# Half of the output projection's early products between the last attention steps, and the attention's PSUM pool kept through the projection

## The chip, the cores and the metric

The kernel runs on one core of one Trainium2 chip. The time of a run is the device time of one execution in microseconds (us); lower is better. A core has a matrix engine (TensorE, "PE" in the profile), a vector engine (VectorE, "DVE"), an activation engine (ScalarE, "ACT"), a general engine (GpSimd, "POOL") and a queue engine that mostly starts transfers (SyncE, "SP"). Each takes its own instructions strictly in the order of its queue. Matrix products land in PSUM, which has eight banks; one bank holds 512 float32 values in each of 128 partitions.

## The reference

One decoder block on 1024 tokens of width 1024: eight heads of attention with forgetting beside a gated chunk mixer, an output projection with a residual, and a gated MLP with a causal convolution of width 3.

```python
def block(x):
    xn = rmsnorm(x, norm_mix_g)
    proj = xn @ w_in                      # q, k, v, u, v_gate, forget logits
    att = forgetting_attention(q, k, v, log_sigmoid(f + b_forget))   # 8 heads of 64
    sg = chunked_spatial_gating(gelu(u), gelu(v_gate), ...)
    h = x + concat(att, sg) @ w_out       # the output projection
    h = h + conv_ffn(rmsnorm(h, norm_ffn_g), w_up, conv_w, conv_b, w_down)
    return rmsnorm(h, norm_final_g)
```

The half of `w_out` that belongs to `sg` is multiplied during the attention, and its sum with `x` is kept in the DRAM buffer `hpd`. What follows the attention is the other half, `att @ w_out[:512]`, which is called the projection here.

## The kernel before

**Number format.** Each float32 operand is split into a high and a low part, and each product is three matrix instructions: high by high, high by low, low by high (L1279, L1280, L1281 in `wmm`). A split is a cast (high) and a subtraction (low).

**Stages.** Attention goes head by head, h = 0 to 7, in five steps each (`STEPS`, n = 5h + s, so n = 35 to 39 are the last head's values). In a step PE transposes probabilities (L1026), ACT and DVE split them (L1027, L1028), PE multiplies them with the values (L1042), and ACT and DVE take the values out of PSUM (L1050, L1051). The logits of the next head are made in the same steps (L978, L979) and read by DVE (L991). The order of PE's attention instructions is chained by hand through `seq`; the rest is put in order by a scheduler, engine by engine, by its own estimates.

**The row tail of a head.** The reciprocals of a head's row sums (`rs`) are transposed by PE (L940), copied by ACT (L941), written to the DRAM buffer `rsd` (L942) and loaded again, spread over partitions, by SP (L943). With them `pair_half` normalizes two heads at a time into `attT[k]`, k = 0 to 3: a multiplication (L952 on POOL, L956 on DVE for the last pair), a cast (L953) and a subtraction (L954, L958). The last pair, k = 3, needs the last head.

**The projection.** `wo_load` fetches the four pieces of `w_out` and POOL splits them (L1098, L1099; buffers `whl` for k = 0, 1 and `G` for k = 2, 3). For the token tiles 0, 4, 1 and 5 (`first`) the products over k = 0, 1, 2 are made ahead, 8 tiles of one bank (`banks8`) by 9 instructions, 72 in all: these are the early products. Then, for each token tile in the order 0, 4, 1, 5, 2, 3, 6, 7: `hload` fetches the tile of `hpd` (SP, L1285, into a buffer `pt`), k = 3 follows (or all of k for tiles 2, 3, 6, 7), `hadd` adds bank and tile on DVE (L1289), `norm2` takes the mean square on ACT (L1296, L1297), the reciprocal (L1298) and the scaled tile `xn` on DVE (L1299), and one tile later `flip` transposes `xn` on PE into two banks (L1317). A flip of tiles 0 to 3 is split (ACT L1306, DVE L1303) and copied (ACT L1323); a flip of tiles 4 to 7 is taken out by one copy on ACT (L1328) and two subtractions on DVE (L1329, L1330), and combined further (L1331, L1334).

**The up stage** multiplies sums of quarter blocks (`xB`, `xT`) with the MLP's weights in 12 instructions per bank (L1372). Its first four products, `qa`, stand around `flip(7)`. DVE splits the weights of these first products (L166) right after the last pair's normalization.

**Banks.** A PSUM pool belongs to a stage. `psb`, the attention's, gives two tiles of two banks each for logits (`place()`, tag "L", taken in turn) and four single banks (`bank()`). In the kernel before it is released right after the attention, and the pool of the projection and of the up stage, `psc`, is made of two groups of four single banks (`bank()` and `sbank()`): the early products lie in all eight, flips in `sbank()`, and the up stage's products in both. A tile of a new pool waits for whoever last used the bank.

Of the kernel before, what the change touches and what calls it, by code (L numbers as in the profile page):

```python
# [14 lines left out]
P = 128  # L15
# [54 lines left out]
def block_kernel(ctx: ExitStack, tc: tile.TileContext, xT, xtok, wuv, wv0, wva, wvk, wvl, wqk, cpk, bfv,  # L70
# [1030 lines left out]

    STEPS = [[(h, g) for g in GROUPS[n:n + 2]] for h in range(8) for n in range(0, 9, 2)]
# [35 lines left out]
    for n, step in enumerate(STEPS):  # L1138
# [3 lines left out]
        if h == 7 and s == 0:  # L1142
            for _ in filler:
                pass
            wo_load((0, 1))
            wo_load((2, 3))
        if h in (2, 4, 6) and s == 4:
            for o in (slice(0, 512), slice(512, 1024)):
                pair_half(h // 2 - 1, o)
        now, turned = turned, [turn_p(g) for g in STEPS[n + 1]] if n + 1 < len(STEPS) else []  # L1150
# [25 lines left out]
        fill((h, s))  # L1176
        for _ in range(min(len(SPLIT), 1 if n == 9 else 2)):
            ws_, k, wr = SPLIT.pop(0)
            wt = sb("whl", [P, 2, 512], F32R)
            ws_[k] = wt  # L1180
            after(tc, act.copy(wt[:, 0], wr), out_copy or casts[-1])
            pool.tensor_tensor(out=wt[:, 1], in0=wr, in1=f32(wt[:, 0]), op=ALU.subtract)
# [19 lines left out]
    psa.release()  # L1202
    psa = tc.alloc_tile_pool(name="psc", bufs=4, space=bass.MemoryType.PSUM, reuse_waits="tile")
# [71 lines left out]
    def wmm(tt, hf, ps, ks_):  # L1275
        ts_ = slice(tt * P, (tt + 1) * P)
        for k in ks_:
            w = wo[k][hf]
            pe.matmul(ps, attT[k][:, 0, ts_], w[:, 0, :], start=(k == 0), stop=False)  # L1279
            pe.matmul(ps, attT[k][:, 0, ts_], w[:, 1, :], start=False, stop=False)  # L1280
            pe.matmul(ps, attT[k][:, 1, ts_], w[:, 0, :], start=False, stop=(k == 3))  # L1281

# [26 lines left out]
    def flip(tt):  # L1309
# [3 lines left out]
        for kh in range(2):  # L1313
            ps = sbank()
            for j in range(4):
                k = 4 * kh + j
                pe.transpose(ps[:, j * P:(j + 1) * P], xn[tt][:, k * P:(k + 1) * P], ident)  # L1317
            pp.append(ps.rearrange("p (k t) -> p k t", k=4))
# [44 lines left out]
    for n in ("T1", "T4", "B22"):  # L1363
        xb_tile(upr, n)

# [15 lines left out]
    for i in range(AHEAD):  # L1381
# [4 lines left out]
        if i == 0:  # L1386

            last = flip(7)
# [430 lines left out]
```

## Time and profile before

| | |
|---|---|
| median of 3 runs | 1050.03 us (1049.67 to 1050.81) |
| the profiled execution | 1049.46 us; its span, first to last instruction, 1047.7 us |
| busy over the span | PE 1038.1, DVE 892.0, ACT 562.3, POOL 218.7 us |
| last head's steps end, early products begin (PE) | 360.78 us from the span's start |
| first product of the up stage (PE) | 410.22 us |
| granted TensorE clock, mean | 0.999 |

Rows of the timeline read: start in us from the span's start, duration in us, engine, line, operation, output and inputs by the program's names, partitions x elements, type, count, and in brackets the idle time of the engine just before, with what ended it. Matrix instructions are pipelined, so that the duration of one overlaps the next; the distance between two starts is what one costs. Rows of the windows give, for a stretch of time, the busy time of each engine with the number of instructions in parentheses, then the granted clock of PE, the share of the transfer engines and GB/s.

### The profile page before, as it was taken

The numbers are of one execution on the slowest core, as the hardware profiler recorded it, in microseconds if no ns is written. First come the engines' busy times: TensorE is split into PE (matmuls) and PEld (weight loads), VectorE is DVE, ScalarE is ACT, GpSimd is POOL, SyncE is SP. The second block draws the span as 40 slices with busy tenths as digits, with TensorE's granted clock in tenths as the row PEclk, the third lists the DMA queues.
The fourth block names the chain that finished last, engine by engine and source line by source line (L and its number), as shares of the span: only waits on it lengthen the run. The fifth ranks groups of instructions, "written<-read, shape, count | busy, mean of one in ns | idle before, by whom it ended". The sixth has DMA issues, their size and how long they took to land.

```text
span 1047.7 us, 14269 instructions
## 1 busy us (share of the span) xinstructions
PE 1038.1 (99%) x4998; PEld 869.6 (83%) x4998; DVE 892.0 (85%) x1302; ACT 562.3 (54%) x1003; POOL 218.7 (21%) x165
## 2 busy tenths in 40 slices
PE   9999999999999999999999999999999999999997
PEld 6988888988888888788888888888888888888886
DVE  6899887888888779998999989898997866997774
ACT  6777632457767747744444444444444544454654
POOL 0000241500422540353334323323331000000000
PEclk9999999999999999999999999999999999999999
DMA  9622558785745533232254431432422999333432
GB/s 323 236 91 86 159 154 252 222 256 172 206 137 171 189 134 141 80 105 77 98 173 162 130 124 60 132 120 70 131 81 81 319 331 303 105 99 101 144 118 100
DMA packets 67452, 161.66 MB, mean 154 GB/s; under 512 B 8095, under 2 KB 9239, under 8 KB 67381
## 3 DMA queue, kind: packets, MB, share of 16 engines
q1 hardware_dynamic: 67108, 160.72, 47.8%
q8 instruction: 39, 0.64, 0.3%
q14 instruction: 33, 0.26, 0.1%
q10 hardware_dynamic: 272, 0.04, 0.0%
HBM read 115.68 MB, written 45.05 MB: 153 GB/s over the span
## 4 chain that ended last, share of the span: by engine, by line
PE 87%; DVE 4%; DMA 3%; ACT 3%; issue 1%; POOL 1%; SPq 0%; ACTq 0%; DVEq 0%; POOLq 0%
PE k L1632 20%; PE qc L1372 11%; PE qa L1372 11%; PE qd L1372 11%; PE qb L1372 5%; PE pb L1042 3%; PE ps L270 3%; PE pb L1026 2%; PE qc L510 2%; PE qa L510 2%; PE pb L270 2%; PE qd L510 2%; PE pl L979 2%; PE pl L978 2%; PE pf L1066 1%; PE pf L1067 1%
## 5 line engine op out<-in xcount | busy, mean ns | idle before, releaser
L1632 PE MATMUL k<-whb,wha 128*128 128x512 f32 (+1 forms) x936 | 209.9, 387 | 0.0
L1632 PEld LDWEIGHTS k<-whb,wha 128*128 128x128 f32 x936 | 174.1, 188 | 35.9 <-DVE wha L166 0.2
L1372 PE MATMUL qc<-xT,whb 128*128 128x512 f32 x540 | 129.8, 389 | 0.2 <-ACT whb L160 0.2
L1372 PE MATMUL qa<-xB,wha 128*128 128x512 f32 x528 | 127.4, 390 | 0.0
L1372 PEld LDWEIGHTS qc<-xT,whb 128*128 128x128 f32 x540 | 101.3, 188 | 21.6 <-ACT whb L160 0.6
L1372 PEld LDWEIGHTS qa<-xB,wha 128*128 128x128 f32 x528 | 98.8, 188 | 20.8 <-DVE wha L166 0.4
L160 ACT CAST wha<-sg 128x512 fp32r<-128x512 f32 x77 | 47.7, 621 | 96.8 <-PE k L1632 83.8
L160 ACT CAST whb<-sg 128x512 fp32r<-128x512 f32 x82 | 50.6, 618 | 87.5 <-PE qc L1372 67.3
L166 DVE TENSOR_TENSOR wha<-sg,wha 128x512 fp32r<-128x512 f32 x77 | 52.9, 690 | 38.9 <-ACT wha L160 38.6
L1372 PE MATMUL qd<-xB,whb 128*128 128x512 f32 x264 | 63.7, 389 | 0.0
L1372 PE MATMUL qd<-xT,whb 128*128 128x512 f32 x264 | 63.7, 390 | 0.0
L1372 PE MATMUL qb<-xT,whb 128*128 128x512 f32 x252 | 61.0, 390 | 0.0
L166 DVE TENSOR_TENSOR whb<-sg,whb 128x512 fp32r<-128x512 f32 x82 | 57.1, 698 | 4.4 <-ACT whb L160 4.3
L1027 ACT CAST pt<-pb 128x512 fp32r<-128x512 f32 x72 | 40.4, 584 | 37.5 <-PE pb L1026 32.5
L1256 POOL TENSOR_TENSOR sg<-raw 128x512 f32<-128x512 f32 x20 | 31.2, 1561 | 140.3 <-DVE whb L166 79.9
L1372 PEld LDWEIGHTS qd<-xT,whb 128*128 128x128 f32 x264 | 49.5, 188 | 10.5 <-DVE u L1479 0.3
L1372 PEld LDWEIGHTS qd<-xB,whb 128*128 128x128 f32 x264 | 49.6, 188 | 10.3
L1028 DVE TENSOR_TENSOR pt<-pb,pt 128x512 fp32r<-128x512 f32 x72 | 47.4, 688 | 10.6 <-ACT pt L1027 10.3
L1372 PEld LDWEIGHTS qb<-xT,whb 128*128 128x128 f32 x252 | 47.2, 188 | 10.0 <-DVE whb L166 0.3
L1042 PE MATMUL pb<-pt,V 128*128 128x512 f32 (+3 forms) x192 | 49.6, 362 | 0.4 <-DVE pt L1028 0.3
L1259 POOL TENSOR_TENSOR sg<-sg,raw 128x512 f32<-128x512 f32 x20 | 33.3, 1667 | 63.4 <-DVE whb L166 63.4
L1257 POOL TENSOR_TENSOR sg<-sg,raw 128x512 f32<-128x512 f32 x20 | 34.8, 1742 | 47.5 <-issue 44.9
(424 smaller groups left out, 2242.9 us busy)
## 6 DMA issues: line engine op xcount, KB each, us to landing
raw<-wup SPq DMA_DIRECT2D x44, 512.0 KB
sg<-hx SPq DMA_DIRECT2D x77, 256.0 KB
hx<-hs SPq DMA_DIRECT2D x44, 256.0 KB
hx<-ca SPq DMA_DIRECT2D x35, 256.0 KB
xT<-wdn SPq DMA_DIRECT2D x28, 256.0 KB
x<-kd SPq DMA_DIRECT2D x24, 256.0 KB
A<-xtok SPq DMA_DIRECT2D x8, 512.0 KB
raw<-wqk SPq DMA_DIRECT2D x8, 512.0 KB
```

Source lines behind the costliest of these rows:

```text
L160: act.copy(h, src)
L166: return eng.tensor_tensor(out=l, in0=src, in1=f32(h), op=ALU.subtract)
L270: pe.matmul(banks[m], xs(n, xi, k)[:, ms], w[:, wi, :], start=(first and k == 0 and c == 0 and (own or m % 2 == 0)), stop=(k == 3 and c == ...
L510: pe.matmul(ps, w[:, wi, ks], xs(n, xi, k), start=(first and c == 0), stop=(c == 11), skip_group_check=True)
L1027: casts.append(act.copy(pt[:, 0, :], ptr))
L1028: los.append(dve.tensor_tensor(out=pt[:, 1, :], in0=ptr, in1=f32(pt[:, 0, :]), op=ALU.subtract))
L1042: seq(pe.matmul(po[half][:, o:o + w], lhs, pt[:, s, c:c + w], start=(new and s == 0), stop=(s == 1 and (half, k) in ((1, 6), (0, 3))), ski ...
L1256: pool.tensor_tensor(out=s[0], in0=a21, in1=a22, op=ALU.add)
L1257: pool.tensor_tensor(out=s[1], in0=s[0], in1=a11, op=ALU.add)
L1259: pool.tensor_tensor(out=s[3], in0=s[1], in1=a12, op=ALU.add)
L1372: pe.matmul(ps, w[:, wi, ks], xb[:, xi, k, :], start=(first and n == 0), stop=(n == 11), skip_group_check=True)
L1632: pe.matmul((banks[bk + m] if ps is None else ps)[:, o], xh[:, xi, ms], wh[:, wi, o], start=((first and p_ == 0 or new) and n == 0), stop= ...
```

## The change

Half of the early products, those of token tiles 0 and 4 (36 of 72 instructions), are issued inside the attention's last steps, n = 34 to 38, by a table `EARLY`: each entry is (token tile, half, pieces k). They are chained into PE's order by `seq`. Their banks are the logits' two wide tiles, which the last logits have left by then. The pieces k = 0, 1 of `w_out` are loaded two steps earlier (n = 33 in place of 35), and k = 2, 3 one step earlier (n = 34). The pool `psb` is kept until the projection is over: the early products of tiles 1 and 5 and all later ones use its four single banks, a flip uses a wide tile in place of two single banks, and `psc` is made only before the first up product. `flip(7)` gets two banks of `psc`.

```diff
+    def wmm(tt, hf, ps, ks_, order=lambda m: m):
+        ts_ = slice(tt * P, (tt + 1) * P)
+        for k in ks_:
+            w = wo[k][hf]
+            order(pe.matmul(ps, attT[k][:, 0, ts_], w[:, 0, :], start=(k == 0), stop=False))
+            order(pe.matmul(ps, attT[k][:, 0, ts_], w[:, 1, :], start=False, stop=False))
+            order(pe.matmul(ps, attT[k][:, 1, ts_], w[:, 0, :], start=False, stop=(k == 3)))
+
+    EARLY = {34: ((0, 0, (0, 1)), (0, 1, (0, 1))), 35: ((4, 0, (0, 1)),), 36: ((4, 1, (0, 1)),),
+             37: ((0, 0, (2,)), (0, 1, (2,))), 38: ((4, 0, (2,)), (4, 1, (2,)))}
+    wide, banks8 = {}, {}
...
-        if h == 7 and s == 0:
+        if n == 33:
             for _ in filler:
                 pass
             wo_load((0, 1))
-            wo_load((2, 3))
         if h in (2, 4, 6) and s == 4:
             for o in (slice(0, 512), slice(512, 1024)):
                 pair_half(h // 2 - 1, o)
+        if n == 34:
+            wo_load((2, 3))
...
         fill((h, s))
+        for tt, hf, ks_ in EARLY.get(n, ()):
+            if tt not in wide:
+                wide[tt] = place()
+            banks8[tt, hf] = wide[tt][:, hf * 512:hf * 512 + 512]
+            wmm(tt, hf, banks8[tt, hf], ks_, seq)
...
     early.release()
-    psa.release()
-    psa = tc.alloc_tile_pool(name="psc", bufs=4, space=bass.MemoryType.PSUM, reuse_waits="tile")
...
-    def flip(tt):
+    def flip(tt, two=None):
 
         c = slice((tt % 4) * P, (tt % 4) * P + P)
         pp = []
-        for kh in range(2):
-            ps = sbank()
+        if two is None:
+            t = place()
+            two = [t[:, 0:512], t[:, 512:1024]]
+        for kh, ps in enumerate(two):
...
     first = (0, 4, 1, 5)
-    banks8 = {(tt, hf): (bank() if hf == 0 else sbank()) for tt in first for hf in range(2)}
     for hf in range(2):
-        for tt in first:
+        for tt in first[2:]:
+            banks8[tt, hf] = bank()
             wmm(tt, hf, banks8[tt, hf], (0, 1, 2))
...
     for n in ("T1", "T4", "B22"):
         xb_tile(upr, n)
+    psa.release()
+    psa = tc.alloc_tile_pool(name="psc", bufs=4, space=bass.MemoryType.PSUM, reuse_waits="tile")
...
-            last = flip(7)
+            last = flip(7, [sbank(), sbank()])
```

In the changed kernel the lines lie a little lower: the three products of `wmm` are L1106 to L1108, `hload` L1293, `hadd` L1297, the mean square, root, reciprocal and scaling of `norm2` L1304 to L1307, the subtraction of a split L1311, the transposes of a flip L1327, its copies L1333 and L1338, its subtractions L1339 and L1340, and the up stage's product L1384.

Three places show what moves. First, PE in the last head's steps. The names are `pb`, a single bank, `pl`, a wide tile, `pt`, the split probabilities, `V`, the values, `whl` and `A`, the pieces of `w_out` and of the attention's output. Before, values of one step are followed at once by the transposes of another:

```order
L1042 MATMUL pb_3759<-pt_3692,V_1733 128x512 x2
L1042 MATMUL pb_3759<-pt_3700,V_1733 128x512 x2
L1026 MATMUL pb_3766<-ident,H_3600 128x128 x2
L1026 MATMUL pb_3766<-ident,H_3563 128x128 x2
L1026 MATMUL pb_3774<-ident,H_3600 128x128
L1026 MATMUL pb_3774<-ident,H_3563 128x128 x3
```

In the changed kernel:

```order
L1042 MATMUL pb_3772<-pt_3722,V_1733 128x512 x2
L1042 MATMUL pb_3772<-pt_3730,V_1733 128x512 x2
L1106 MATMUL pl_3779<-whl_3656,A_2849 128x512
L1107 MATMUL pl_3779<-whl_3656,A_2849 128x512
L1108 MATMUL pl_3779<-whl_3656,A_2849 128x512
L1106 MATMUL pl_3779<-whl_3664,A_3281 128x512
L1107 MATMUL pl_3779<-whl_3664,A_3281 128x512
L1108 MATMUL pl_3779<-whl_3664,A_3281 128x512
L1026 MATMUL pb_3786<-ident,H_3600 128x128 x2
L1026 MATMUL pb_3786<-ident,H_3563 128x128 x2
```

Six early products of token tile 4 stand between; five such groups are put in, of 12, 6, 6, 6 and 6 instructions.

Second, PE at the end of the projection, where `flip(6)`, `flip(7)` and the first up products (`qa`) stand. Before:

```order
L1280 MATMUL pb_4270<-G_3738,G_3837 128x512
L1281 MATMUL pb_4270<-G_3738,G_3837 128x512
L1372 MATMUL qa_4318<-xB_3859,wha_3870 128x512 x3
L1317 MATMUL ps_4290<-ident,xn_4232 128x128 x4
L1317 MATMUL ps_4295<-ident,xn_4232 128x128 x4
L1372 MATMUL qa_4318<-xB_3859,wha_3870 128x512 x9
L1372 MATMUL qa_4331<-xB_3860,wha_3873 128x512 x12
L1317 MATMUL ps_4344<-ident,xn_4284 128x128 x4
L1317 MATMUL ps_4349<-ident,xn_4284 128x128 x4
L1372 MATMUL qa_4371<-xB_3859,wha_3956 128x512 x12
```

In the changed kernel:

```order
L1107 MATMUL pb_4258<-G_3716,G_3875 128x512
L1108 MATMUL pb_4258<-G_3716,G_3875 128x512
L1327 MATMUL pl_4278<-ident,xn_4221 128x128 x8
L1384 MATMUL qa_4309<-xB_3893,wha_3904 128x512 x12
L1384 MATMUL qa_4322<-xB_3894,wha_3907 128x512 x12
L1327 MATMUL ps_4335<-ident,xn_4272 128x128 x4
L1327 MATMUL ps_4336<-ident,xn_4272 128x128 x4
L1384 MATMUL qa_4362<-xB_3893,wha_3950 128x512 x12
```

The three products ahead of `flip(6)` now stand behind it, and `flip(6)` lies in the wide tile `pl_4278`. Its two banks are the first of `psc`, and the first product, `qa_4309`, takes the first of them.

Third, DVE around the scaled tile of `norm2(6)`. Before (`xn_4232` is that tile, `ps_4238` and `ps_4243` the banks of `flip(3)`, `ps_4290` one of `flip(6)`):

```order
L1303 TENSOR_TENSOR xB_3859<-ps_4238,xB_3859 128x4x128
L1303 TENSOR_TENSOR xB_3860<-ps_4243,xB_3860 128x4x128
L1289 TENSOR_TENSOR pt_4254<-pb_4256,pt_4254 128x512
L1298 RECIPROCAL ss_3845<-ss_3845 128x1
L1299 SCALAR_TENSOR_TENSOR xn_4232<-pt_4202,ss_3845,g2b 128x1024
L1289 TENSOR_TENSOR pt_4254<-pb_4270,pt_4254 128x512
L1329 TENSOR_TENSOR xtB_3863<-xtB_3863,ps_4290 128x4x128
L1330 TENSOR_TENSOR t_703_4300<-xtB_3865,ps_4290 128x512
L1298 RECIPROCAL ss_3845<-ss_3845 128x1
```

In the changed kernel (`xn_4221` is that tile, `pl_4227` the wide tile of `flip(3)`, `pl_4278` that of `flip(6)`):

```order
L1297 TENSOR_TENSOR pt_4242<-pb_4244,pt_4242 128x512
L1311 TENSOR_TENSOR xB_3893<-pl_4227,xB_3893 128x4x128
L1306 RECIPROCAL ss_3883<-ss_3883 128x1
L1307 SCALAR_TENSOR_TENSOR xn_4221<-pt_4191,ss_3883,g2b 128x1024
L1311 TENSOR_TENSOR xB_3894<-pl_4227,xB_3894 128x4x128
L1297 TENSOR_TENSOR pt_4242<-pb_4258,pt_4242 128x512
L1339 TENSOR_TENSOR xtB_3897<-xtB_3897,pl_4278 128x4x128
L1306 RECIPROCAL ss_3883<-ss_3883 128x1
L1340 TENSOR_TENSOR t_694_4287<-xtB_3899,pl_4278 128x512
```

The second subtraction of `flip(3)`'s split (`xB_3894`) moved behind the scaled tile, and the reciprocal of `norm2(7)` ahead of the subtraction L1340 that reads `flip(6)`.

More of the change, by code (lines that the diff above doesn't have):

```diff
@@ L1273, in block_kernel @@
     normed = {}
[L1275 to L1281, printed above, removed]
     def hload(tt):
```

## The prediction

> **What bounds the kernel now.** I read the page first: the totals and the chain of waits.
>
> ```profile
> span 1047.7 us, 14269 instructions
> PE 1038.1 (99%) x4998; PEld 869.6 (83%) x4998; DVE 892.0 (85%) x1302; ACT 562.3 (54%) x1003; POOL 218.7 (21%) x165
> PE 87%; DVE 4%; DMA 3%; ACT 3%; issue 1%; POOL 1%; SPq 0%; ACTq 0%; DVEq 0%; POOLq 0%
> ```
>
> PE is busy for 1038.1 of 1047.7 us. The change moves matrix instructions and adds none, so it can only win idle time of PE, and it loses whatever idle time it makes. The table by windows says where PE is idle near the change:
>
> ```profile
> 350.00:355.00 5.00, 4.11 (x31) 3.46 (x30) 4.29 (x10) 4.49 (x12) 5.00 (x6) 1.00 0.59 181
> 355.00:360.00 5.00, 4.94 (x32) 3.84 (x30) 3.42 (x7) 3.68 (x9) 0.55 (x1) 1.00 0.48 161
> 360.00:365.00 5.00, 4.72 (x23) 3.95 (x23) 2.08 (x4) 2.23 (x4) 0.00 (x0) 1.00 0.94 269
> ```
>
> Idle by these rows: 0.89 + 0.06 + 0.28 = 1.23 us. Busy time includes the modelled tails of instructions, so PE has more room than that. The timeline of PE over the last head's steps and the projection shows how much:
>
> ```profile
> 350.94 0.62 PE L1026 MATMUL pb<-ident,H 128*128 128x128 f32 x4
> 352.46 0.66 PE L1026 MATMUL pb<-ident,H 128*128 128x128 f32 x4 [0.90 <-DVE pt L1028]
> ...
> 360.78 0.45 PE L1279 MATMUL pb<-whl,A 128*128 128x512 f32 x1
> ...
> 377.17 0.39 PE L1279 MATMUL pb<-G,G 128*128 128x512 f32 x1
> ...
> 384.31 0.47 PE L1280 MATMUL pb<-whl,A 128*128 128x512 f32 x1
> 384.62 0.40 PE L1281 MATMUL pb<-whl,A 128*128 128x512 f32 x1
> ...
> 410.22 0.84 PE L1372 MATMUL qa<-xB,wha 128*128 128x512 f32 x3
> 410.92 1.06 PE L1317 MATMUL ps<-ident,xn 128*128 128x128 f32 x8
> 411.74 5.04 PE L1372 MATMUL qa<-xB,wha 128*128 128x512 f32 x21
> ```
>
> From 360.78 to 377.17 stand the 72 early products: 16.39 / 72 = 0.2276 us each. Eight transposes take 411.74 - 410.92 = 0.82, 0.10 each. The first product after transposes takes 384.62 - 384.31 = 0.31, 0.08 more than another.
>
> **The gain at the attention's end.** From 350.94 to 360.78, 9.84 us, PE issues 29 transposes (2.9 us by 0.10) and values that amount to 18 products of 512 columns (4.1), with six changes from the one to the other (0.5): 7.5 us of work, so 2.3 us of room. That is above the 1.23 of the windows and is my value; the rows bound the gain between 1.2 and 2.7 (without the changes). The 36 moved products are 36 x 0.2276 = 8.2 us, enough to fill it. Two conditions must hold. The bank must be free and the pieces of the output weights split by then:
>
> ```profile
> 350.40 0.53 DVE L991 CUSTOM_DVE_ANT_0 gg<-pl,t,lim 128x256 f32<-128x256 f32 x1
> ...
> 334.68 1.29 POOL L952 TENSOR_TENSOR H<-H 128x512 f32<-128x512 f32 x1 [30.00 <-DVE H L1051]
> 336.18 0.61 POOL L953 CAST G<-H 128x512 fp32r<-128x512 f32 x1 [0.21 <-PE pf L1068]
> ```
>
> DVE leaves the wide bank at 350.93, and the first group starts then. On POOL the changed order puts two multiplications, four casts, a cast of the pair and four subtractions up to the last split of k = 0, 1; that is six operations of 1.29 and five of 0.61 us at most from 334.68, an end by 345.5, 5 us early. So both hold, and the last values end about 5.9 us later (8.2 - 2.3) instead of 8.2. The remaining 36 products follow, and PE leaves them at 374.8 instead of 377.17, 2.3 us ahead.
>
> **Where most of that lead goes.** The same groups stand ahead of the row tail (L940) and of the values that free the buffer for the first residual tile. SP and DVE show what hangs on these:
>
> ```profile
> 359.23 0.33 SPq L1285 DMA_DIRECT2D pt<-hpd  x1
> 360.12 0.45 SPq L943 DMA_DIRECT2D H<-rsd  x1
> ...
> 364.57 1.29 DVE L956 TENSOR_TENSOR H<-H 128x512 f32<-128x512 f32 x2 [2.29 <-DMA H<-rsd]
> ...
> 367.17 4.68 DVE L166 TENSOR_TENSOR wha<-raw,wha 128x512 fp32r<-128x512 f32 x4
> 378.05 0.69 DVE L1289 TENSOR_TENSOR pt<-pb,pt 128x512 f32<-128x512 f32 x1 [6.20 <-PE pb L1281]
> ...
> 382.06 1.28 DVE L1299 SCALAR_TENSOR_TENSOR xn<-pt,ss,g2b 128x1024 f32<-128x1024 f32 x1
> ```
>
> Thirty moved products (6.8 us) stand ahead of those values, less some 2 us of idle time: both loads of SP's queue go out 4.8 us later, the row sums land at 369.4, and DVE's L956, L958 and the four L166 (7.28 us from 364.57 to 371.85) end at 376.7. Before, DVE was idle for 6.20 us there, which hid this work; now it is late itself, and the first `hadd` starts at 376.7, only 1.35 ahead of 378.05. The roots of tiles 0 and 4 are taken together on ACT, which costs another 0.7, so the first scaled tile starts near 381.5 against 382.06. PE waits for it at `flip(0)`, and later for the bank of tile 5, since four single banks now serve where eight did. I take 0.6 us of lead behind these waits, bounded by 0.2 and 1.2.
>
> **The new wait.** At the end of the projection the first up product takes a bank of `flip(6)`, since the new pool starts there. It must wait until ACT's copy and DVE's L1340 (before: L1330) have read it. Before, it stood ahead of that flip in another bank, and 21 products followed the flip. The rows, DVE first:
>
> ```profile
> 405.26 0.68 DVE L1303 TENSOR_TENSOR xB<-ps,xB 128x512 fp32r<-128x512 f32 x1
> 405.87 1.28 DVE L1289 TENSOR_TENSOR pt<-pb,pt 128x512 f32<-128x512 f32 x2
> ...
> 409.49 1.28 DVE L1299 SCALAR_TENSOR_TENSOR xn<-pt,ss,g2b 128x1024 f32<-128x1024 f32 x1
> ...
> 413.07 0.69 DVE L1330 TENSOR_TENSOR t<-xtB,ps 128x512 f32<-128x512 f32 x1 [0.79 <-ACT xtB L1328]
> 413.67 0.16 DVE L1298 RECIPROCAL ss<-ss 128x1 f32<-128x1 f32 x1
> 413.75 0.67 DVE L1331 TENSOR_TENSOR t<-xtB,xtB 128x512 f32<-128x512 f32 x1
> ```
>
> and ACT:
>
> ```profile
> 405.98 0.59 ACT L1323 COPY xtB<-ps 128x512 f32<-128x512 f32 x1 [2.75 <-DVE xB L1303]
> 406.46 1.08 ACT L1306 CAST xB<-ps 128x512 fp32r<-128x512 f32 x2
> ...
> 411.41 1.06 ACT L1296 ACTIVATE xn<-pt 128x1024 f32<-128x1024 f32 x1 [1.68 <-DVE pt L1289]
> ...
> 412.47 0.57 ACT L1328 COPY xtB<-ps 128x512 f32<-128x512 f32 x1
> 412.94 0.29 ACT L1297 ACTIVATE ss<-ss,eps 128x1 f32<-128x1 f32 x1
> ```
>
> In the changed order, from the end S of the scaled tile of `norm2(6)`: DVE's second split of `flip(3)` 0.61 (405.87 - 405.26), now behind the scaled tile; ACT's two copies of that flip, queued behind the split, 2 x 0.48 = 0.96; the square of tile 7, 1.06 (412.47 - 411.41); the copy L1338, 0.57; root and reciprocal of tile 7, now ahead of L1340, 0.19 (to 413.23) and 0.08; L1340 itself, 0.69; six hand-offs between engines of 0.05 to 0.15, such as ACT to DVE from 413.04 to 413.07. Sum 4.16 + 0.5 = 4.7 us. PE's `flip(6)` runs under it, S + 0.2 to S + 1.0, and then PE has nothing: 3.7 us idle.
>
> S was 409.49 + 1.28 = 410.77 and becomes 410.2 by the lead. The first product starts at 414.9. Before, with its three products put behind the flip, the same point is 411.74 - 3 x 0.2276 = 411.05. So PE leaves this place 3.85 us late. Behind it the up stage is bound by PE and returns nothing, except that its feeding engines get time: I give 0.3 for small waits further on. Sum +3.5. The profiled execution, 1049.46, becomes 1053.0; its median of runs lies 0.57 higher, so **1053.5 us**.
>
> **Hidden edits.** The earlier weight loads lie under POOL's 30.00 us of waiting. Keeping the old pool costs no instruction. The two-bank flip has the same eight transposes; its price is that both halves are given back together, which I have charged at the end only.
>
> **The rivals.**
>
> *Contention, a larger loss.* POOL's sums of later weights follow the last L166 and now run under the scaled tiles of tiles 0 and 4, where DVE is the late engine.
>
> ```profile
> 367.93 1.67 POOL L1251 TENSOR_TENSOR raw<-raw,raw 128x512 f32<-128x512 f32 x1 [12.38 <-DVE wha L166]
> 438.50 1.71 DVE L1422 SCALAR_TENSOR_TENSOR cg<-h,cp,cg 128x1023 f32<-128x1023 f32 x1 [0.54 <-ACT cg L1421]
> 445.20 1.27 DVE L1424 SCALAR_TENSOR_TENSOR ca<-h,cp,ca 128x1022 f32<-128x1022 f32 x1
> ```
>
> The operation of L1299 took 1.71 beside a busy POOL and 1.27 without. Four such operations lose 4 x 0.44 = 1.8 us, and the 0.6 us of lead goes with them at most: 1055.
>
> *The clock falls in the new gap.* PE has no gap above 0.90 us in the rows above, and the granted clock is 1.00 in all of them. The only long rest in the trace is the start:
>
> ```profile
> 1.29 3.58 PE L126 MATMUL ps<-gg 128*128 128x512 bf16 x8 [1.29 <-DVE pad L137]
> 4.85 3.81 PE L270 MATMUL pb<-wy,V 128*128 128x512 f32 x13
> ```
>
> Those first eight products of 512 columns took (4.85 - 1.29) / 8 = 0.445 us each, against 0.2276 later. If 3.7 us of rest bring that back, about eight products lose 0.22 each: +1.7, 1055.2. Against it: no row shows it in the middle of a run, and the gap must be long enough. [...]
>
> *About the same.* The lead of 2.3 is mostly kept, and the wait is as short as the same distance was before, from `flip(6)`'s first transpose to the end of L1330: 413.76 - 410.92 = 2.84, less 0.82 of transposes, 2.0. Then -2.3 + 2.0 = -0.3, 1049.7. For it: ACT may take its copies earlier than the queue order makes me think. Against: the split ahead of these copies stands behind the scaled tile in DVE's queue.
>
> *Faster, the other side.* The new pool's first product does not wait at all, because the reads of the bank end under PE's own queue; then the full 2.3 stays and 1047.7 results. It decides once L1340 ends within 1 us of the flip. The sum of ACT's square and copy alone (1.63) speaks against it.
>
> *The change does not fill the gap*, because the pieces are not split in time: PE then waits inside the attention, the 2.3 is lost and the end wait stays, 1054 to 1056. The margin of 5 us speaks against it.
>
> **How the numbers follow.** Forecast 0.65, contention 0.10, clock 0.07, not filled 0.03, about the same 0.08, faster 0.07. The forecast's own range, from a lead of 1.2 and no hand-off cost to a lead of 0.2 and late hand-offs, is 1052.3 to 1054.6. To hold 8 in 10 I go up to 1055.6, over contention and clock, and down to 1050.6, part of the way to no change. About 0.2% (2.1 us) is what a measurement of this kernel tells from no change: slower is the forecast and the three larger losses, less a share of the forecast that ends below +2.1, 0.78; the same 0.12; faster 0.10, since "about the same" may land beyond either bound.
>
> **What would show it.** Right: PE rows from 351 to 366 without a gap above 0.3 us; L956 near 369.4 and the first `hadd` near 376.7; at about 411 a gap of 3 to 4 us on PE ahead of the first up product, ended by DVE's L1340. Wrong: L956 near 365 (the lead is kept), a first up product right behind `flip(6)`, a granted clock below 1.00 or products 0.44 us apart after the gap, or a matrix instruction of the early groups that waits for POOL.

## The result and the profile after

| | before | changed |
|---|---|---|
| median | 1049.85 us, 4 runs (1049.00 to 1050.81) | 1059.40 us, 4 runs (1058.85 to 1060.38) |
| ratio, 95% interval | | 1.0096 (1.0084 to 1.0108) |
| profiled execution | 1049.46 us | 1059.03 us |
| its span | 1047.7 us | 1057.3 us |
| granted TensorE clock, mean | 0.999 | 0.996 |

The changed kernel is slower by 1%: +9.6 us of span, where +3.5 had been forecast. It lies outside the predicted range. First the page of the changed kernel: its totals and the shares of its chain of waits.

```profile
span 1057.3 us, 14267 instructions
PE 1040.4 (98%) x4998; PEld 871.8 (82%) x4998; DVE 895.9 (85%) x1302; ACT 562.4 (53%) x1003; POOL 218.0 (21%) x165
PE 87%; DVE 6%; DMA 3%; issue 1%; ACT 1%; SPq 1%; DVEq 0%; ACTq 0%
```

PE's busy time grew by 2.3 us though its 4998 instructions are the same, so some of them became slower; idle time grew by 9.6 - 2.3 = 7.3 us; and DVE's share of the chain rose from 4% to 6%. The table of PE's waits says for whom (engine, line and what it waited for; us in total, times, longest):

```profile
PE qa L1384 <- DVE t L1340: 3.5, 1, 3.5
PE qc L1384 <- DVE u L1495: 2.1, 1, 2.1
PE pl L1327 <- DVE xn L1307: 2.0, 3, 1.0
```

The first is the forecast wait for `flip(6)`'s bank. The second, in the up stage, was not forecast. The third is the projection's flips. The timeline of PE shows these places one after the other:

```profile
374.87 0.39 PE L1106 MATMUL pl<-G,G 128*128 128x512 f32 x1
...
384.12 1.09 PE L1327 MATMUL pl<-ident,xn 128*128 128x128 f32 x8 [1.00 <-DVE xn L1307]
...
412.12 1.06 PE L1327 MATMUL pl<-ident,xn 128*128 128x128 f32 x8 [0.36 <-DVE xn L1307]
416.73 8.04 PE L1384 MATMUL qa<-xB,wha 128*128 128x512 f32 x24 [3.54 <-DVE t L1340]
424.61 1.03 PE L1327 MATMUL ps<-ident,xn 128*128 128x128 f32 x8
...
469.09 2.88 PE L1384 MATMUL qd<-xT,whb 128*128 128x512 f32 x12
474.03 3.02 PE L1384 MATMUL qc<-xT,whb 128*128 128x512 f32 x12 [2.06 <-DVE u L1495]
```

From it the 9.6 us are summed. The first up product starts at 416.73 against 411.05 before (the three products ahead of `flip(6)` counted behind it, as in the prediction): **+5.7**. The first 24 products, which go 0.2276 us apart before and so take 5.46, take 424.61 - 416.73 = 7.88: **+2.4**. At the point where PE takes up 12 products of `qa` (466.37, before 459.14) the distance is 7.2, so 0.9 has come back on the way. Then comes the second stall, **+2.1**, and 0.3 in small waits.

The table by windows shows the slow products (columns as before: busy time of PE, its weight loads, DVE, ACT and POOL, then the granted clock, the transfers' share and GB/s):

```profile
350.00:355.00 5.00, 5.00 (x30) 4.26 (x29) 2.97 (x9) 3.03 (x8) 5.00 (x6) 1.00 0.34 105
...
415.00:420.00 5.00, 3.27 (x8) 2.63 (x9) 4.77 (x8) 3.65 (x9) 0.00 (x0) 0.50 0.06 24
420.00:425.00 5.00, 5.00 (x22) 4.01 (x21) 1.38 (x3) 1.11 (x3) 0.00 (x0) 0.83 0.02 3
```

In the last steps of the attention PE is now busy all the time (the next two rows, up to 365, read 5.00 as well); behind the wait its granted clock is 0.50 and it issues 8 products in the time of 14.

Where the 5.7 us come from is seen on DVE:

```profile
369.46 1.29 DVE L956 TENSOR_TENSOR H<-H 128x512 f32<-128x512 f32 x2 [1.34 <-DMA H<-rsd]
...
376.66 1.27 DVE L1297 TENSOR_TENSOR pt<-pl,pt 128x512 f32<-128x512 f32 x2
...
381.73 2.34 DVE L1307 SCALAR_TENSOR_TENSOR xn<-pt,ss,g2b 128x1024 f32<-128x1024 f32 x1
...
384.18 2.11 DVE L1307 SCALAR_TENSOR_TENSOR xn<-pt,ss,g2b 128x1024 f32<-128x1024 f32 x1
...
410.69 1.28 DVE L1307 SCALAR_TENSOR_TENSOR xn<-pt,ss,g2b 128x1024 f32<-128x1024 f32 x1
411.89 0.68 DVE L1311 TENSOR_TENSOR xB<-pl,xB 128x512 fp32r<-128x512 f32 x1
...
415.23 0.69 DVE L1339 TENSOR_TENSOR xtB<-xtB,pl 128x512 f32<-128x512 f32 x1 [2.06 <-ACT xtB L1338]
415.84 0.15 DVE L1306 RECIPROCAL ss<-ss 128x1 f32<-128x1 f32 x1
415.91 0.67 DVE L1340 TENSOR_TENSOR t<-xtB,pl 128x512 f32<-128x512 f32 x1
```

and on ACT between the last of these:

```profile
412.61 1.07 ACT L1333 COPY xtB<-pl 128x512 f32<-128x512 f32 x2 [1.64 <-DVE xB L1311]
413.56 1.07 ACT L1304 ACTIVATE xn<-pt 128x1024 f32<-128x1024 f32 x1
...
414.62 0.58 ACT L1338 COPY xtB<-pl 128x512 f32<-128x512 f32 x1
```

The scaled tile of tile 6 ends at S = 410.69 + 1.28 = 411.97, where 410.2 was forecast and 410.77 stood before. From there to PE's first product it is 416.73 - 411.97 = 4.76 us, through the split, the two copies, the square, the last copy and the two subtractions L1339 and L1340. Two earlier scaled tiles, of tiles 0 and 4, took 2.34 and 2.11 us instead of 1.28, and POOL is at work beside them:

```profile
381.70 1.29 POOL L1269 TENSOR_TENSOR raw<-raw 128x512 f32<-128x512 f32 x1
382.94 2.26 POOL L1275 TENSOR_TENSOR raw<-sg,raw 128x512 f32<-128x512 f32 x1
```

The second of these is longer too, by 2.26 - 1.29 = 0.97 us. DVE's 2.34 is its own 1.28 and 1.06 more, nearly the 1.26 for which POOL's first operation of these two still runs (381.73 to 382.99). By what means the one holds up the other, no row shows.

The second stall, on DVE in the changed kernel and then at the same place before:

```profile
467.25 1.78 DVE L166 TENSOR_TENSOR whb<-sg,whb 128x512 fp32r<-128x512 f32 x1
468.96 0.68 DVE L1491 TENSOR_TENSOR u<-qb,u 128x512 f32<-128x512 f32 x1
469.56 2.08 DVE L1436 SCALAR_TENSOR_TENSOR ca<-h,cp,ca 128x1022 f32<-128x1022 f32 x1
471.56 0.68 DVE L166 TENSOR_TENSOR whb<-sg,whb 128x512 fp32r<-128x512 f32 x1
...
473.30 0.67 DVE L1495 TENSOR_TENSOR u<-u,qc 128x512 f32<-128x512 f32 x1
```

```profile
459.48 0.68 DVE L1479 TENSOR_TENSOR u<-qb,u 128x512 f32<-128x512 f32 x1
...
463.45 0.68 DVE L1483 TENSOR_TENSOR u<-u,qc 128x512 f32<-128x512 f32 x1
```

and PE's product that needs the bank, before:

```profile
464.58 2.88 PE L1372 MATMUL qc<-xT,whb 128*128 128x512 f32 x12
```

Before, the subtraction that frees the bank ended at 464.13, 0.45 us ahead of the product that needs the bank (464.58). Now it ends at 473.97 and PE stands from 471.97. The edit touches none of these lines. The scheduler gave DVE another order in the up stage: one more weight split (L166) ahead of the two subtractions. It does not lie between them, where both kernels have the same three operations. Counted from the L1491 of the unit before (449.51, before 442.37) to L1495, DVE does nine splits where it did eight, and it is 2.7 us longer under way: 0.6 for the extra split, and the rest because two of the nine, at 459.74 and 467.25, take 1.77 and 1.78 us beside a busy POOL, where such a split takes 0.68.

### The profile page after: what moved, and what is told of

Read it like the earlier page. It is cut to its first block, busy times and chain, and to the rows that moved or that the text cites. A ratio compares the mean times of both kernels' runs of the same rounds, so it can differ in the third digit from the quotient of the medians.

```text
span 1057.3 us, 14267 instructions
## 1 busy us (share of the span) xinstructions
PE 1040.4 (98%) x4998; PEld 871.8 (82%) x4998; DVE 895.9 (85%) x1302; ACT 562.4 (53%) x1003; POOL 218.0 (21%) x165
## 4 chain that ended last, share of the span: by engine, by line
PE 87%; DVE 6%; DMA 3%; issue 1%; ACT 1%; SPq 1%; DVEq 0%; ACTq 0%
PE k L1644 20%; PE qa L1384 11%; PE qc L1384 11%; PE qd L1384 10%; PE qb L1384 5%; PE ps L270 5%; PE pb L270 4%; PE pb L1042 3%; PE pb L1026 3%; PE qc L510 2%; PE pl L979 2%; PE pl L978 2%; PE qd L510 2%; PE qa L510 2%; PE pf L1066 1%; PE pf L1068 1%
## 5 line engine op out<-in xcount | busy, mean ns | idle before, releaser
L1384 PE MATMUL qa<-xB,wha 128*128 128x512 f32 x528 | 129.6, 395 | 3.5 <-DVE t L1340 3.5
L1384 PE MATMUL qc<-xT,whb 128*128 128x512 f32 x540 | 129.9, 389 | 2.1 <-DVE u L1495 2.1
L1384 PEld LDWEIGHTS qa<-xB,wha 128*128 128x128 f32 x528 | 100.5, 191 | 25.2 <-issue 3.7
L1384 PEld LDWEIGHTS qc<-xT,whb 128*128 128x128 f32 x540 | 101.3, 188 | 23.5 <-DVE u L1495 2.5
L166 DVE TENSOR_TENSOR wha<-sg,wha 128x512 fp32r<-128x512 f32 x77 | 52.8, 688 | 39.2 <-ACT wha L160 39.1
L1384 PE MATMUL qd<-xB,whb 128*128 128x512 f32 x264 | 63.7, 389 | 0.0
L1384 PE MATMUL qd<-xT,whb 128*128 128x512 f32 x264 | 63.4, 389 | 0.0
L166 DVE TENSOR_TENSOR whb<-sg,whb 128x512 fp32r<-128x512 f32 x82 | 58.2, 710 | 4.4 <-ACT whb L160 4.3
L1384 PE MATMUL qb<-xT,whb 128*128 128x512 f32 x252 | 60.9, 389 | 0.0
L1384 PEld LDWEIGHTS qd<-xB,whb 128*128 128x128 f32 x264 | 49.6, 188 | 10.3
L1384 PEld LDWEIGHTS qd<-xT,whb 128*128 128x128 f32 x264 | 49.6, 188 | 10.3
L1384 PEld LDWEIGHTS qb<-xT,whb 128*128 128x128 f32 x252 | 47.3, 188 | 9.8
```

What stands on the lines that cost most here:

```text
L166: return eng.tensor_tensor(out=l, in0=src, in1=f32(h), op=ALU.subtract)
L1384: pe.matmul(ps, w[:, wi, ks], xb[:, xi, k, :], start=(first and n == 0), stop=(n == 11), skip_group_check=True)
```

## The experiments

Four causes were to be told apart: the wait for the bank, the clock behind it, the contention with POOL, and DVE's order in the up stage. Each kernel is the changed one with the edit shown. In the table the second column is the start of the first up product less 411.05, the third what low clock cost, the fourth PE's later waits for DVE in the up stage, all of the profiled execution; their sum should come near the difference of the spans.

| kernel | first up product | clock | later waits | sum | span less 1047.7 | median (range, runs) | ratio to before |
|---|---|---|---|---|---|---|---|
| changed | +5.7 | 2.4 | 2.1 | 10.2 | 9.6 | 1059.40 (1058.85–1060.38, 4) | 1.0096 (1.0084–1.0108) |
| e1_banks | +2.0 | 1.7 | 1.5 + 2.1 | 7.3 | 6.9 | 1056.17 (1055.55–1056.66, 4) | 1.0065 (1.0049–1.0082) |
| e2_fill | +6.3 | 0 | 2.0 | 8.3 | 7.8 | 1057.86 (1057.00–1060.04, 4) | 1.0086 (1.0071–1.0101) |
| e3_pool_only | +4.4 | 1.7 | 2.1 | 8.2 | 7.5 | 1057.22 (1056.93–1059.53, 4) | 1.0081 (1.0066–1.0096) |
| e4_few | +4.1 | 2.9 | 2.0 | 9.0 | 8.4 | 1057.73 (1057.40–1057.82, 4) | 1.0081 (1.0066–1.0096) |
| e6_order | +1.8 | 0 | 1.5 + 0.6 | 3.9 | 3.7 | 1054.43 (1053.16–1054.75, 5) | 1.0040 (1.0027–1.0053) |
| e7_few_all | -1.0 | 0 | 1.5 + 0.6 | 1.1 | 1.1 | 1050.63 (1050.34–1051.96, 10) | 1.0011 (1.0002–1.0021) |
| e9_best | -1.0 | 0 | 1.6 + 0.9 | 1.5 | 1.4 | 1050.85 (1049.93–1053.99, 11) | 1.0017 (1.0008–1.0026) |
| e10_none | +0.2 | 0 | 1.6 + 0.8 | 2.6 | 2.4 | 1051.67 (1050.82–1052.27, 11) | 1.0021 (1.0013–1.0030) |
| e11_copies | -0.6 | 0 | 0.6 + 0.6 | 0.6 | 0.5 | 1050.10 (1049.00–1051.30, 11) | 1.0007 (0.9998–1.0017) |
| e12_b22 | +1.2 | 0 | 0.2 + 0.6 | 2.0 | 1.9 | 1049.65 (1049.00–1051.30, 11) | 1.0003 (0.9994–1.0012) |

The sums are 0 to 0.7 us above the differences of the spans; the rest is small waits elsewhere that come and go. The runs of the kernel before that stood beside them had medians of 1049.1 to 1049.3 us. e8_hold is not in the table: its profiled execution, 1060.53, lies 3.8 us above its other three.

**e1_banks** takes the wait for `flip(6)`'s bank away: the two banks of `flip(7)` are taken first from the new pool, so that they are the ones `flip(6)` had, and the first up product gets another.

```diff
+    seven = [sbank(), sbank()]
...
-            last = flip(7, [sbank(), sbank()])
+            last = flip(7, seven)
```

> The changed kernel, except that the two banks of flip(7) are taken first from the new pool, so that the first up product gets a bank that flip(6) does not hold. Theory: the wait for DVE's L1340 (3.5 us of PE idle ahead of the first up product) is gone, with it the low clock behind it (24 products in 5.5 us and not 7.9), so about 3.7 + 2.4 us less than the changed kernel: 1053.3 us, and 1051 if the later 2.1 us stall of PE at 472 us goes with it. Rival: the loss comes from the projection having four single banks and two wide tiles in place of eight banks, or from the delayed row sums; then the time stays above 1057.

PE's timeline in e1_banks:

```profile
413.00 5.72 PE L1385 MATMUL qa<-xB,wha 128*128 128x512 f32 x24
...
435.70 0.97 PE L1385 MATMUL qb<-xT,whb 128*128 128x512 f32 x3 [1.50 <-DVE whb L166]
...
469.88 4.61 PE L1385 MATMUL qc<-xT,whb 128*128 128x512 f32 x12 [2.08 <-DVE u L1496]
```

The first product follows `flip(6)` at once and its 24 take 5.56 us: the wait and the low clock behind it are gone, 6.05 us together (424.61 - 418.56). The median fell by 3.2 only. 1.5 us came back as a new wait of `qb` for a weight split on DVE, and the clock fell behind the second stall instead: there 12 products took 4.45 us in place of 2.72, +1.7. So the wait is shown to be the bank's, and DVE is shown to be late right behind it. The median stands 2.9 us above the expected 1053.3.

**e2_fill** keeps the wait and puts 12 idle products into it, whose result is overwritten.

```diff
+                if dummies:
+                    after(tc, m, dummies.pop())
...
+            if i == j == 0:
+                seven = [sbank(), sbank()]
+                for m in range(12):
+                    x = pe.matmul(seven[0], attT[3][:, 0, 0:P], wo[3][0][:, 0, :], start=True, stop=True)
+                dummies.append(x)
...
-            last = flip(7, [sbank(), sbank()])
+            last = flip(7, seven)
```

> The changed kernel with 12 idle products (their result is overwritten) on PE between flip(6) and the first up product, in a bank that is free; the wait for L1340 itself stays. Theory: the clock falls because PE rests for 3.5 us; with 2.7 us of it filled, the first up product starts at the same time (416.7 us, within 0.4), and the first 24 take 5.5 us in place of 7.9 at a granted clock of 1.00: 1057.0 us. Rival: these products are slow for another reason (their operands, or the wait of the weights); then 7.9 us and 1059.4 us stay.

PE's timeline in e2_fill:

```profile
413.57 3.00 PE L1401 MATMUL ps<-G,G 128*128 128x512 f32 x12
417.37 5.69 PE L1384 MATMUL qa<-xB,wha 128*128 128x512 f32 x24 [0.80 <-DVE t L1340]
```

In this execution the rest of 3.54 us is 0.80 now, the granted clock is 1.00 throughout, and the 24 products take 5.52 us (to 422.89) instead of 7.88. The low clock is thus shown to be the consequence of the rest. The profiled execution gained 1.8 us; the median gained 1.5, with runs that overlap with those of the changed kernel.

**e3_pool_only** keeps the attention's pool, the two-bank flips and the earlier loads of `w_out`, but makes all 72 early products after the attention, as before. **e4_few** moves 12 of them (those of tile 0) instead of 36.

```diff
-    EARLY = {34: ((0, 0, (0, 1)), (0, 1, (0, 1))), 35: ((4, 0, (0, 1)),), 36: ((4, 1, (0, 1)),),
-             37: ((0, 0, (2,)), (0, 1, (2,))), 38: ((4, 0, (2,)), (4, 1, (2,)))}
+    EARLY = {}
```

In e4_few that line is:

```diff
+    EARLY = {34: ((0, 0, (0, 1)),), 35: ((0, 1, (0, 1)),)}
```

The products that are not in the table are made where all 72 stood before, tile 4's into a wide tile.

> The changed kernel with all 72 early products behind the attention, as before; the attention's banks are still kept through the projection. Theory: no gain at the attention's end, no late row sums (L956 near 364.6, scaled tile of tile 0 near 382 at 1.3 us), but the same wait ahead of the first up product (about 3.5 us of idle) and the same low clock (2.4 us): 1056 to 1059 us. Rival: the banks cost nothing and the moved products are the loss: 1050 us.

> The changed kernel with 12 of the 36 moved products (token tile 0, k = 0 and 1, ahead of the row tail) inside the attention and the other 24 behind it. Theory: 12 products (2.7 us) fill the idle 2.3 us, the row sums come at most 0.7 us later than before (L956 near 365) and the scaled tiles of tiles 0 and 4 take 1.3 us, not 2.1 to 2.3, so that PE stays 1 to 2 us ahead up to flip(6); the wait and the low clock at the up stage stay: 1054 to 1057 us. Rival: the delayed row sums cost nothing: 1059 us as the changed kernel.

PE in e3_pool_only:

```profile
415.48 7.29 PE L1388 MATMUL qa<-xB,wha 128*128 128x512 f32 x24 [3.54 <-DVE t L1339]
```

With no product moved at all the kernel is 7.5 us of span behind, with the same bank wait of 3.54, the same low clock and the same second stall. So it is not the moved products that cost most of the time but the pool that was kept for them, with the clock and the second stall that come with it. In both kernels the scaled tiles of tiles 0 and 4 take 1.28 again, since POOL's sums end at 379.3 and 381.5; so the contention of the changed kernel is shown to come from the delay that the moved products bring, and it is worth about 1.4 us: from the start of the first scaled tile to S it is 30.24 us in the changed kernel, 28.84 in e3_pool_only and 28.80 in e4_few. That the profiled execution of e4_few is no faster than that of e3_pool_only, though its first product starts 0.4 earlier, is the clock: 24 products took 8.34 us in the one and 7.13 in the other. The median of e4_few, 1057.73, lies above the expected 1054 to 1057; the two kernels' runs overlap.

**e6_order** is e1_banks with two weight splits of the fourth unit of the up stage (S2 and S3) placed behind the two subtractions of the third unit that PE waits for.

```diff
+        if i == 2:
+            gates["S2"], gates["S3"] = m2, m3
```

> The kernel e1_banks (the changed kernel with the bank wait taken away) with one more rule for DVE's queue: in the up stage's third unit the low halves of the next unit's S2 and S3 weights stay behind the two subtractions (L1491, L1495 in the changed kernel) that PE waits for, so that as many weight splits stand ahead of them as in the kernel before. Theory: the 2.1 us stall of PE at 468 us comes from the one weight split more that the scheduler put ahead of them (0.7 us, 1.8 beside a busy POOL); the stall falls to 0.5 us or less, and the low clock behind it (1.7 us) goes: 1052.3 to 1053.3 us against 1056.2 of e1_banks. Rival: DVE is late there from work that piled up before, whatever the order; then 1055.5 us or more.

PE's timeline in e6_order:

```profile
468.27 3.01 PE L1387 MATMUL qc<-xT,whb 128*128 128x512 f32 x12 [0.61 <-DVE u L1498]
```

The second stall fell from 2.08 to 0.61 us and the clock stayed at 1.00; the median fell by 1.7, though not to the expected 1053.3 or less. Eight splits stand ahead of the subtraction again, and only one of them takes 1.78 us. So DVE's order is shown to be the cause of 1.5 of the 2.1 us. The wait of `qb`, 1.5, stayed.

**e7_few_all** joins e4_few, e1_banks and e6_order, and both halves of k = 3 of tiles 0 and 4 are made ahead of their additions.

```diff
-                hadd(tt, hf, banks8[tt, hf])
+                if tt in (1, 5):
+                    hadd(tt, hf, banks8[tt, hf])
+                elif hf == 1:
+                    hadd(tt, 0, banks8[tt, 0])
+                    hadd(tt, 1, banks8[tt, 1])
```

> All the remedies in one: 12 products inside the attention (e4_few), the first up product in a bank that flip(6) does not hold (e1_banks), the DVE rule of e6_order, and for token tiles 0 and 4 both halves of k = 3 ahead of their additions. Theory: e1_banks' 1056.2 less the 1.6 us that flip(6) came earlier in e4_few, less 2.1 and 1.7 of the second stall and its clock: 1050.8 us, the kernel before within 0.3%, and not faster, because DVE and ACT set the pace of the projection. Rival: keeping the lead of 2 us, 1048.5 us.

The first product starts at 410.10, 0.95 us ahead of the kernel before, so here the filled idle time arrives at the end of the projection. Still the kernel is 0.1% slower, and the wait of `qb` of 1.5 us eats the lead.

**e8_hold** is e1_banks with POOL's sums held back until the scaled tile of tile 4 is done, against the contention.

```diff
+        if tt == 4:
+            for y in held:
+                tc.add_manual_dep(y.ins, normed[4].ins.name, ...)
```

> The kernel e1_banks with POOL's sums of the next weights held until the scaled tile of token tile 4 is written; the queues' orders are the same. Theory: the scaled tiles of tiles 0 and 4 took 2.34 and 2.11 us because POOL worked beside them; now both take 1.28, and flip(6) starts 1 to 1.9 us earlier: 1054.3 to 1055.2 us against 1056.2. Rival: the overlap only moves to the next scaled tiles and additions, and nothing is won: 1056 us.

Its median, 1056.73 us (1056.66 to 1060.53), is 0.6 above e1_banks. In its profiled execution the scaled tiles of tiles 0 and 4 took 1.28, but that of tile 1 now met POOL, as DVE's row shows:

```profile
388.22 2.28 DVE L1309 SCALAR_TENSOR_TENSOR xn<-pt,ss,g2b 128x1024 f32<-128x1024 f32 x1
```

The rival was right: the collision moved by one tile and further on. Held back, the sums run from 385.6 to 397.9, under work that DVE is also late with: L1343 and L1346, 0.68 and 0.69 in the changed kernel (there L1341 and L1344), take 1.81 and 1.75, and PE waits 1.90 and 2.01 us for banks that DVE's additions free. So no run takes the contention away alone; its price rests on the comparison with e3_pool_only and e4_few.

**e9_best** is e7_few_all with the wait of `qb` attacked, by giving that product's splits an earlier place in DVE's queue, and with both splits of the fourth unit held behind the second of the two subtractions; **e10_none** is the same with no product moved into the attention.

```diff
-            gates["S2"], gates["S3"] = m2, m3
+            gates["S2"], gates["S3"] = m3, m3
...
+    WB[1](("S2",))
...
-        wb(("S2",))
+        if i > 0:
+            wb(("S2",))
```

> The kernel e7_few_all with two more rules for the up stage's splits: the second unit's S2 weights are split ahead of the first unit's A22 and S4, and the S2 and S3 of the fourth unit both stay behind the two subtractions that PE waits for. Theory: in e7_few_all PE still waits 1.5 us for the first and 0.6 us for the second; both go, so 1050.6 - 2.1 = 1048.5 us, 0.1% under the kernel before. Rival: DVE's backlog moves the wait to the next product and the time stays at 1050 us or more.

> The kernel e9_best without any product inside the attention: all 72 early products stand behind it, and DVE's queue is the same. It prices the moved products alone, with the later waits out of the way. Theory: 12 products in the idle time at the attention's end are worth what flip(6) comes earlier by them, 0.4 (e3_pool_only to e4_few) to 1.6 us: e9_best plus 0.4 to 1.6. Rival: the projection's pace is set by DVE and ACT alone, so e9_best within 0.3 us.

PE's timeline in e9_best:

```profile
434.00 3.02 PE L1398 MATMUL qc<-xT,whb 128*128 128x512 f32 x12 [1.58 <-DVE u L1509]
...
446.72 3.01 PE L1398 MATMUL qc<-xT,whb 128*128 128x512 f32 x12 [0.87 <-DVE u L1509]
```

In e9_best `qb` no longer waits, and the next bank's subtraction comes 1.58 us late instead: here the order within DVE's queue only chooses who waits, and the median stays at 1050.85 where 1048.5 was expected. Against e10_none, the 12 moved products start the up stage 1.14 us earlier (409.28 against 410.42 for `flip(6)`) and are worth 0.8 us in the medians. The gain of filling the attention's idle time is real and of about that size, though the two kernels' runs overlap.

**e11_copies and e12_b22** ask why DVE is late. In e7_few_all DVE has no pause from 412.39 to 436.35, and in the kernel before none from 413.07 to 436.24, above 0.1 us. DVE at the split that `qb` waits for, in e7_few_all and then in the kernel before:

```profile
412.39 0.69 DVE L1340 TENSOR_TENSOR xtB<-xtB,pl 128x512 f32<-128x512 f32 x1 [2.06 <-ACT xtB L1339]
...
432.07 0.68 DVE L166 TENSOR_TENSOR whb<-sg,whb 128x512 fp32r<-128x512 f32 x1
```

```profile
431.96 0.69 DVE L166 TENSOR_TENSOR whb<-sg,whb 128x512 fp32r<-128x512 f32 x1
```

The split stands at the same time in both, although PE is 0.95 us ahead in the one. That stretch of some 23 us is DVE's, and it begins with the subtractions on `flip(6)`, which wait for ACT's copies of `flip(3)`, which wait for DVE's second split of it. e11_copies makes those copies first; e12_b22 also puts the copy of `flip(6)` ahead of the square of tile 7.

```diff
+        if tt == 3:
+            hl_of("B11", c, pp[0])
+            for n, p3 in (("B11", pp[0]), ("B21", pp[1])):
+                y = act.copy(xt[n][:, :, c], p3)
+                after(tc, y, rooted[6])
+            x = act.copy(XB["B21"][:, 0, :, c], pp[1])
+            after(tc, x, y)
+            lo_of("B21", c, pp[1])
+            return
```

and in e12_b22 also:

```diff
-        act.copy(b22, pp[1])
+        y = act.copy(b22, pp[1])
+        if tt == 6:
+            after(tc, squared[7], y)
```

> As e7_few_all, but ACT makes the two copies of flip(3) right behind the root of tile 6 and ahead of the second cast of that flip; in e7_few_all the copies stood behind DVE's second split of it. In e7_few_all DVE is without a break from 413.0 to 435.6 us, as it is in the kernel before from 413.1, and the split that PE's qb waits for ends at 432.75 against 432.65 before, though PE is 0.95 us ahead there. Theory, DVE's queue: the lead is lost because DVE starts that stretch no earlier, held for 2.06 us by the copies of flip(3). With the copies early, the first subtraction on flip(6) starts near 410.5 in place of 412.39, the second one only near 412.4 (it waits for the copy behind the square of tile 7) in place of 413.07; DVE gains 0.7 us, the wait of qb falls from 1.5 to about 0.8, the span from 1048.8 to about 1048.1, the median to 1049.9. Rival, the split at qb waits for its own cast or weights and not for DVE's queue: qb's wait stays at 1.5 and the median at 1050.6.

> As e11_copies, and ACT's copy of flip(6)'s second bank stands ahead of the square of tile 7. Theory, DVE's queue: both subtractions on flip(6) run from about 410.5 to 411.8; DVE gains 1.3 to 2 us on e7_few_all, qb's wait goes to 0 to 0.3, what is left of later waits is about 0.6 on u, and the span is 1047.2 to 1047.8, the median 1049.0 to 1049.6: no longer slower than the kernel before. Rival as for e11_copies: qb still waits 1.5 and the median is 1050.6. A second rival: DVE gains but the wait moves to the next product that needs a split or a subtraction (as in e9_best), and the median is 1050.2 to 1050.8.

PE in e11_copies:

```profile
432.18 0.97 PE L1407 MATMUL qb<-xT,whb 128*128 128x512 f32 x3 [0.59 <-DVE whb L166]
```

The wait of `qb` is 0.59 in e11_copies (forecast 0.8) and 0.24 in e12_b22 (0 to 0.3), and the medians, 1050.10 and 1049.65, are where the theory of DVE's queue put them or within 0.2 us. The first subtraction came at 411.78, not near 410.5 as expected, since it waits for the copy of `flip(6)` too. The profiled execution of e12_b22 began its work 1.5 us late, in waits of the first stage, and is 1.65 above its median; the start of its first product is to be read with that. e12_b22 can't be told from the kernel before: ratio 1.0003 (0.9994 to 1.0012). No version was faster than it.

## Why the prediction was right and wrong

**The gain at the attention's end** held. The remaining 36 products leave PE at 374.87 us (forecast 374.8), the windows from 350 to 365 are full, and by e9_best against e10_none a third of these products alone is worth 0.8 to 1.1 us.

**Where most of that lead goes** had the right mechanism and a wrong sign. The row sums land at 369.46 (369.4), the first addition starts at 376.66 (376.7), the first scaled tile at 381.73 (381.5). But of the 0.6 us of lead said to be left nothing was: S came 1.2 us later than before, not 0.6 earlier. Of the difference of 1.8, 0.3 is a smaller lead (the first scaled tile starts 0.33 ahead of 382.06), and about 1.4 is the rival **contention**, in which two scaled tiles lost 2.34 + 2.11 - 2 x 1.28 = 1.9 us, some of it made up again up to S. That its price of 1.8 came so near is luck: it was worked out as four operations at 0.44 each, and came as two, at 1.06 and 0.83. It was given a chance of 0.10 although the sum itself had DVE late at that place and POOL's sums moved under it.

**The new wait** was right in place and size: 4.76 us from S to the first product against 4.7, 3.54 us of idle PE against 3.7, ended by L1340. In the path one term was missing, and that the sum still fits is luck: the first subtraction, L1339, also waits for the copy L1338 here and costs 0.61, while the hand-offs came to 0.2 and not 0.5, and the root of tile 7 (0.19) ran beside the path.

**The clock** fell in that wait, at 414.83 us, and cost 2.4 us where the rival had 1.7, because 6.83 us of low clock followed, where the falls that cost 1.7 (e3_pool_only, e1_banks) lasted 3.41. For the eight slow products at the start, from which that price was taken, a low clock is not shown: the windows of the kernel before read 1.00 there from 0 to 5 us, and the trace's record of the clock has its first entry only at 4.73. The chance of 0.07 was the author's estimate, with no row of the trace behind it. In the runs the clock fell within a rest of 3.54 us in the changed kernel and in e4_few (at 414.22), 0.36 us behind one of 3.54 in e3_pool_only, and 0.11 us behind one of 2.08 in e1_banks.

**The step that failed** is the end of the sum: "So PE leaves this place 3.85 us late. Behind it the up stage is bound by PE and returns nothing, except that its feeding engines get time". It has the contention ahead of this place and the low clock behind it at nothing, where 1.8 us (with the smaller lead) and 2.4 were measured, and it has the up stage bound by PE alone. There 0.9 us came back where 0.3 had been given, and then 2.1 were lost. In the kernel before (413.07 to 436.24) and in e7_few_all (412.39 to 436.35) DVE works without a pause at the start of that stage, so it is as much the bound there as PE; in the changed kernel, where PE comes late, it rests 3.86 us once, up to 425.24, and is the bound only further on. The order in which it works is the scheduler's, which a change 50 us ahead rearranged. The prediction compared the orders of DVE around the projection and not in the stage behind it. e6_order and e9_best show that the wait goes where DVE's queue puts it, e11_copies and e12_b22 that it gets shorter when DVE begins that stretch sooner behind `flip(6)`.

**The rivals as alternatives.** The forecast, contention and clock were given chances as if one of them would happen. They stand in a row, and each is a consequence of the one ahead: the delay brings DVE under POOL's sums, and the wait brings PE's rest. 3.85 + 1.8 + 2.4 - 0.9 + 2.1 + 0.3 = 9.6, by terms of which three were written down, the wait and the contention near their sizes and the clock 0.7 too small. The two rivals without a loss had no ground: in all three kernels with the pool kept and the banks as the change has them PE waited for 3.54 us.

Left open: why the scheduler chose the other order, and whether splitting the first up weights ahead of the last pair's normalization, which wasn't tried, would give DVE the missing time.

## What to carry to other kernels

A buffer that is kept longer to fill a gap also keeps its readers: ask who must have read it before the next stage's first write, and price that chain through each engine's queue; here the pool alone, with what followed from it, cost 7.5 us of span, where a third of the moved products was worth about one. Losses that follow from one another are to be added, not weighed as rivals: here the late engine met what ran beside it (a scaled tile took 2.34 us beside POOL's sums, 1.28 without), and in the matrix engine's wait of 3.54 us the granted clock fell to 0.50. Before a lead is counted at the end, look for the next stretch in which another engine works without a pause, for it ends there.

## What the runs showed of the hardware

The granted clock changed in steps of about 3.41 us. It was 0.50 from 414.83 to 421.66 us in the changed kernel (6.83 us), for 6.83 us in e4_few, and for 3.41 in e3_pool_only (415.84 to 419.25) and e1_banks, from 469.99 on. The table by windows, cut at these points, in e1_banks:

```profile
466.58:469.99 3.41, 1.33 (x7) 0.79 (x6) 3.41 (x5) 0.62 (x1) 1.76 (x1) 1.00 0.00 0
...
469.99:473.40 3.41, 3.41 (x9) 2.65 (x10) 2.83 (x3) 0.00 (x0) 1.65 (x2) 0.50 0.41 154
```

and in the changed kernel, first the stretch ahead of the fall and the two of low clock, then two stretches over its second stall, whose border lies 17 steps of 3.413 us after the fall (from 421.66 to the clock's last fall, at 1056.54, it is 634.88 us, 186 such steps):

```profile
411.42:414.83 3.41, 1.40 (x10) 0.86 (x8) 1.75 (x3) 2.22 (x5) 0.00 (x0) 1.00 0.25 98
414.83:418.24 3.41, 1.51 (x4) 1.26 (x5) 3.01 (x5) 2.19 (x5) 0.00 (x0) 0.50 0.14 58
418.24:421.66 3.42, 3.42 (x10) 2.65 (x9) 3.14 (x6) 2.73 (x6) 0.00 (x0) 0.50 0.00 0
```

```profile
469.45:472.86 3.41, 2.52 (x12) 1.75 (x10) 3.41 (x4) 1.56 (x3) 1.60 (x2) 1.00 0.00 0
472.86:476.27 3.41, 2.24 (x10) 1.86 (x11) 3.41 (x5) 0.00 (x0) 2.78 (x2) 1.00 0.41 154
```

The clock fell behind stretches in which PE was busy for 1.33 and 1.40 us of 3.41 and stayed up behind 2.52 and 2.24. So two rests of the same length, 2.08 and 2.06, did different things: the first lay in one stretch, the second was cut in two. No row between the two falls marks the border; that it lies there is inferred from the 186 steps, and no run varied the place of a rest alone. The low clock ended behind a stretch that was wholly busy (e3_pool_only, e1_banks) and went on behind stretches with 1.51 us (the changed kernel) and 2.52 us (e4_few) of work, which is why one fall cost 1.7 us and another 2.4 to 2.9.
